# RMSNorm and matmul: x in a ring of 36 tiles, loaded twelve tiles at a time

## The chip, the core and the metric

The kernel runs on one core of a Trainium2 chip. The metric is the device time of one execution in microseconds (us), as the median of several runs; lower is better. A core has five engines with instruction streams of their own: TensorE (PE in the profile; PEld is its weight load), VectorE (DVE), ScalarE (ACT), GpSimd (POOL) and SyncE (SP, which only issues transfers here). 16 DMA engines move data between the chip's memory and the on-chip buffers (SBUF); the accumulators of TensorE are in PSUM.

## The reference

```python
batch, seq, dim, out_dim = 16, 1024, 512, 768        # x: float32, gamma: ones, eps: 1e-5
rms = np.sqrt(np.mean(x ** 2, axis=-1, keepdims=True) + eps)
x_norm = x / rms * gamma
return np.matmul(x_norm, weight).astype(np.float32)  # weight: [512, 768]
```

Each of the 16,384 rows of x is divided by its root mean square, scaled by gamma, and multiplied by the weight.

## The kernel before, in words

The rows are cut into 128 tiles of 128 rows (NT), taken in 64 pairs j (NP). A tile of x is 2 KB on each of the 128 partitions, a tile of the output 3 KB. The product is computed on the raw x in bf16, with gamma folded into the weight, and each output row is multiplied by its 1/rms when it leaves the accumulator.

Each tile goes through these steps:

- **Load** (`load`, L177). The first 32 tiles come on SP's queue in loads of 2, 2, 4, 8, 8 and 8 tiles, around the two halves of the weight (`load_weights`, L345). The later ones come on ScalarE's queue, 8 tiles (16 KB a partition) each. x has two buffers of 16 tiles, so a load overwrites tiles 32 places back and waits for their readers.
- **Cast** (`cast`, L188) on GpSimd, to bf16, in groups of up to 8 tiles, in `xb` (two buffers of 8 tiles). The last four tiles of each 16 (from tile 28 on) are a *quad*: `cast_quad` (L260) puts them in `xq`.
- **Turn.** TensorE transposes a tile as two blocks of 32-bit words against an identity (`transpose_word`, L230), into two PSUM banks; VectorE copies the result to `xT` (`evac`, L239). A quad is turned by 16 VectorE transposes (`move`, L271), three per pair from the pair after its cast on.
- **Norm.** ScalarE squares each tile and sums it (`square`, L196); a group's `root` is a square root on ScalarE (L201) and a reciprocal on VectorE (L203).
- **Product** (`matmuls`, L296 and L300): four weight loads and eight matmuls a tile, into one of three accumulators. A `feeder` puts the transposes of the pair after next between them.
- **Evict** (`finish_tile`): ScalarE (L279) takes the even tile of a pair and VectorE (L281) the odd one, into `ot`, three output buffers of 8 tiles. The last tile of a group is followed by its **store** (`store`, L293) on SP's queue. The first and last groups are stored in smaller pieces.

`Order` keeps the program's order on each engine and adds the semaphore waits that the named cells require. Every engine works in order, so an instruction that waits holds all that stand behind it. In the loop over pairs, pair j issues the casts of tiles some 8 to 16 places ahead, squares of pair j + 4, and the loads:

```python
if j == START or j > START and (j + LEAD) % 4 == 0:                          # START, LEAD = 4, 14
    load_until(2 * XG + OG if j == START else 2 * (j + LEAD) + OG)           # XG, OG = 16, 8
```

So from pair 6 on, every fourth pair issues the load of the eight tiles that begin at tile 2j + 28.

`rows` says which rows of x and the output a tile holds: within a block of t tiles, partition p holds t rows that lie next to each other in memory, one for each tile of the block. From tile 32 on the block is 32 tiles, so a partition's rows are 64 KB (x) or 96 KB (output) from the next partition's.

Of the kernel before, what the change touches and what calls it, by code (L numbers as in the profile page):

```python
# [11 lines left out]
F32 = mybir.dt.float32  # L12
BF16 = mybir.dt.bfloat16
AF = mybir.ActivationFunctionType


P = 128
# [83 lines left out]
def kernel(  # L101
# [9 lines left out]
    PE, DVE, ACT, POOL, SP = nc.tensor, nc.vector, nc.scalar, nc.gpsimd, nc.sync  # L111
    order = Order(tc)

    def run(engine, issue, reads=(), writes=()):
        order.add(1, engine, issue, reads, writes)

    x = x.flatten_outer_dims()
    out = out.flatten_outer_dims()
    N, D = x.shape
    _, O = out.shape  # L120
    K = D // P
    NT = N // P
    NP = NT // 2
    XG, OG = 16, 8
    FIRST, START, LEAD = 2 * XG, 4, 14

    def stretches(group, parts):
        first, size, i = {}, {}, 0
        for g in range(NT // group):
            for n in parts.get(g, [group]):  # L130
                for t in range(i, i + n):
                    first[t], size[t] = i, n
                i += n
        return first, size

    last = NT // OG - 1
    x_first, x_size = stretches(OG, {0: [2, 2, 4]})
    o_first, o_size = stretches(OG, {0: [1, 1, 2, 4], last - 1: [4, 4], last: [4, 2, 2]})

    def rows(ap, i, n):  # L140
        base, t = (i - i % OG, OG) if OG <= i < XG else (x_first[i], x_size[i]) if i < OG else (i - i % XG, XG) if i < 2 * XG else (i - i % (2 * XG), 2 * XG)
        return ap[base * P:(base + t) * P, :].rearrange("(p t) d -> p t d", t=t)[:, i - base:i - base + n, :]

    def sb(name, shape, dtype):
        return nc.alloc_sbuf_tensor(name, shape, dtype).ap()
# [5 lines left out]
    eps_sb = sb("eps_sb", [P, 1], F32)  # L151
    ident_f = sb("ident_f", [P, P], F32)
    g_sb = sb("g_sb", [P, 2, 2], F32)
    xt = [sb(f"xt{n}", [P, XG, D], F32) for n in range(2)]
    xb = [sb(f"xb{n}", [P, 8, D], BF16) for n in range(2)]
    jk = [sb(f"jk{n}", [P, D], BF16) for n in range(2)]
    xT = [sb(f"xT{n}", [P, 2, 2, P, 2], BF16) for n in range(4)]
# [1 line left out]
    xTq = [sb(f"xTq{n}", [P, 4, 2, P, 2], BF16) for n in range(2)]  # L159
    ot = [sb(f"ot{n}", [P, OG, O], F32) for n in range(3)]  # L160
    ssq = sb("ssq", [P, NT], F32)
    rms = sb("rms", [P, NT], F32)
    rstd = sb("rstd", [P, NT], F32)
    psum = nc.alloc_psum_tensor("ps", [P, 8 * WIDE], F32).ap()
    ops = [psum[:, 2 * WIDE * n:2 * WIDE * (n + 1)] for n in range(3)]
# [2 lines left out]
    def cells(name, slot, i, n=1):  # L168
        return [(name, slot, t) for t in range(i, i + n)]

    def x_of(i, n=1):
        return xt[i // XG % 2][:, i % XG:i % XG + n, :], cells("x", i // XG % 2, i % XG, n)

    def load(i):
        dst, to = x_of(i, x_size[i])
        queue = SP if i < FIRST else ACT
        order.transfer(queue, lambda: queue.dma_start(out=dst, in_=rows(x, i, x_size[i])), writes=to)  # L177
# [3 lines left out]
    def load_until(i):  # L181
        while starts and starts[0] < i:
            load(starts.pop(0))

    def cast(i, n=1):
        src, of = x_of(i, n)
        s = i // 8 % 2
        run(POOL, lambda: POOL.tensor_copy(out=xb[s][:, i % 8:i % 8 + n, :], in_=src), of, cells("xb", s, i % 8, n))  # L188
# [3 lines left out]
    def square(i):  # L192
        src, of = x_of(i)
        j = squares[0] % 2
        squares[0] += 1
        run(ACT, lambda: ACT.activation(out=jk[j], in_=src[:, 0, :], func=AF.Square, accum_out=ssq[:, i:i + 1]),  # L196
            of, [("jk", j), ("ssq", i)])

    def root(i, n):
        s = slice(i, i + n)  # L200
        run(ACT, lambda: ACT.activation(out=rms[:, s], in_=ssq[:, s], func=AF.Sqrt, scale=1.0 / D, bias=eps_sb),  # L201
            [("ssq", t) for t in range(i, i + n)] + ["eps"], [("rms", i)])
        run(DVE, lambda: DVE.reciprocal(out=rstd[:, s], in_=rms[:, s]), [("rms", i)],  # L203
            [("rstd", t) for t in range(i, i + n)])

    def norms(i, n):
        for t in range(n):
            square(i + t)
        root(i, n)
# [6 lines left out]
    def norms_of_group(j):  # L216
        square(2 * j)
        square(2 * j + 1)
        if j in norm_end:
            root(*norm_end[j])  # L220
# [33 lines left out]
    def quad_of(j):  # L254
        return j // 2 if (2 * j) % XG >= XG - 4 and 2 * j >= XG else None

    def cast_quad(q):
        src, of = x_of(4 * q, 4)
        s = 4 * q // XG % 2
        run(POOL, lambda: POOL.tensor_copy(out=xq[s], in_=src), of, [("xq", s)])  # L260
        for t in range(4):
            xT_of[4 * q + t] = (xTq[s][:, t], ("xTq", s))
        words = xq[s].rearrange("p t d -> p (t d)").bitcast(F32).rearrange("p (a w) -> p a w", w=P)
        turned = xTq[s].rearrange("p t h m c -> p (t h m c)").bitcast(F32).rearrange("p (a m) -> p a m", m=P)
        for tokens in range(0, P, B):
            for features in range(0, P, B):
                quad_moves.append((turned[features:features + B, :, tokens:tokens + B],
                                   words[tokens:tokens + B, :, features:features + B], s))
# [4 lines left out]
    def move_quad(n):  # L273
        for _ in range(min(n, len(quad_moves))):
            move(*quad_moves.pop(0))
# [9 lines left out]
    def accumulator():  # L285
        return next(turns) % 3

    def store(i):
        first, n = o_first[i], o_size[i]
        s = first // OG % 3  # L290
        if i == first + n - 1:
            src = ot[s][:, first % OG:first % OG + n, :]
            order.transfer(SP, lambda: SP.dma_start(out=rows(out, first, n), in_=src), reads=cells("ot", s, first % OG, n))  # L293
# [12 lines left out]
    def matmuls(i, a, ks, feed=None):  # L306
        block, cell = xT_of[i]
        for k in ks:
            lhsT = block[:, k // 2, :, k % 2]
            hold(lhsT, cell)  # L310
            for half, lo, hi in ((0, 0, WIDE), (1, WIDE, O)):
                product(ops[a][:, lo:hi], lhsT, w_bf[:, k, lo:hi], k == 0, k == K - 1,
                        [cell, ("w", k, half)], [("ops", a, half)])
            if feed:
                feed()

    def finish_tile(i, a, engine):
        s = i // OG % 3

        before = [("ot", s, i % OG - 1)] if i == o_first[i] + o_size[i] - 1 else []  # L320
        scale(engine, ot[s][:, i % OG, :], ops[a][:, :O], rstd[:, i:i + 1],
              [("ops", a, 0), ("ops", a, 1), ("rstd", i)] + before, [("ot", s, i % OG)])
        store(i)

    def feeder(pairs, gaps, alone=False):
        queue = [(j, t, h) for j in pairs for t in range(2) for h in range(2)]
        calls = iter(gaps)

        def feed():
            for _ in range(next(calls)):  # L330
                j, t, h = queue.pop(0)
                transpose_word(j, t, h)
                if alone and h == 1:
                    evac(j, t, 1)
                elif (t, h) == (1, 1):
                    evac(j)
        return feed
# [37 lines left out]
    for c in range(2):  # L375
        turn_gamma(c)
    run(DVE, lambda: DVE.tensor_copy(out=g_sb.rearrange("p c h -> p (c h)"), in_=tp[0][:, 0, 0, :4]), [("tp", 0)], ["g"])  # L377
    cast(0)
    cast(1)
    cast(2, 2)  # L380
    norms(0, 2)
    warm_up(2)
# [22 lines left out]
    for j in range(1, NP):  # L405
        if j in (1, 2):
            cast(4 * j + 4, 4)
        elif j % 8 == 4 and j + 4 < NP:
            cast(2 * j + 8, 8)
        elif j % 8 == 6 and j + 2 < NP:  # L410
            cast(2 * j + 12, 4)
        if (2 * j + 2) % XG == 0 and 2 * j + 2 < NT:
            cast_quad((2 * j + 2 + XG - 4) // 4)
        elif 2 * j >= XG:
            move_quad(3)
        if j < 4:
            norms(2 * j + 2, 2)
        for pair in norm_turns.get(j, []):
            norms_of_group(pair)
        if j == START or j > START and (j + LEAD) % 4 == 0:  # L420
            load_until(2 * XG + OG if j == START else 2 * (j + LEAD) + OG)
        if j < 3:
            feed = feeder([j + 1], mid if j == 1 else one, alone=j == 1)
        elif j == 3:
            feed = feeder([4, 5], both)
        elif j + 2 < NP and quad_of(j + 2) is None:
            feed = feeder([j + 2], two)
        else:
            feed = None
        for i, engine in ((2 * j, ACT), (2 * j + 1, DVE)):  # L430
            a = accumulator()
            matmuls(i, a, range(K), feed)
            finish_tile(i, a, engine)
# [48 lines left out]
```

## Time and profile before

| | |
|---|---|
| median of three runs | 208.84 us (208.83 to 209.33) |
| the profiled execution: its own time | 209.07 us |
| its span, first to last instruction | 207.1 us |
| granted TensorE clock | 0.993 |
| busy share: TensorE, VectorE, ScalarE, GpSimd | 94%, 72%, 70%, 29% |
| moved by DMA | 85.62 MB, 413 GB/s over the span |
| loads of x past tile 7: median from issue to landing | 18.2 us (3 on SP), 18.8 us (12 on ScalarE) |
| stores of 8 tiles, 3,072 KB: median from issue to landing | 22.7 us (13) |

The span is cut into 40 slices in the page's rows of digits; 9 is busy for 90% of a slice or more. In a list of groups or a timeline, a line names the engine, the line of the program, the operation, the tiles (out<-in) and how often; in brackets stands how long the engine was idle before, and what ended that. The name after an arrow in the list of waits is who was waited for, followed by the total in us, the number of waits and the longest. A DMA is split into packets; here one packet is one partition's row of a transfer, and each of the 16 DMA engines moves 8 of the 128.

### The profile page before, as it was taken

The page shows a single profiled execution, that of the slowest core. Times are in us where ns is not written, and L with a number is a line of the kernel's source. Part 1 is how long each engine was busy: PE and PEld are TensorE (multiplying, and loading weights), DVE is VectorE, ACT ScalarE, POOL GpSimd, SP SyncE. Part 2 cuts the span into 40 slices and gives each one's busy share as a digit, 9 for nine tenths or more (in the row PEclk, how much of TensorE's full clock was granted, in tenths as well). Part 3 has the DMA queues.
Part 4 walks back from the last instruction along what each step waited for, and adds up shares of the span by engine and source line. Part 5 has one row for each costly group of instructions (what it writes and reads, how often), then busy time and mean ns, then how long its engine had stood idle before and what let it go on. Part 6 is the DMA issues. An engine that isn't in the chain of part 4 may idle for free.

```text
span 207.1 us, 2794 instructions
## 1 busy us (share of the span) xinstructions
PE 194.7 (94%) x1236; PEld 72.7 (35%) x717; DVE 149.5 (72%) x255; ACT 144.3 (70%) x343; POOL 60.0 (29%) x34
## 2 busy tenths in 40 slices
PE   7789999999999999999999999999999989999940
PEld 1233434343334334433344333443343324333310
DVE  0446556999579975999579975999569964999530
ACT  4598898777777687777777687676949758683310
POOL 2156752157006340065105170060604224000000
PEclk9999999999999999999999999999999999999997
DMA  6999999999999999999999999999999999999992
GB/s 222 402 434 453 370 419 420 426 461 407 437 429 423 449 419 440 419 434 429 432 449 411 430 434 423 445 423 437 413 424 445 427 440 435 423 437 394 394 412 120
DMA packets 6064, 85.62 MB, mean 413 GB/s; under 512 B 674, under 2 KB 676, under 8 KB 1828
## 3 DMA queue, kind: packets, MB, share of 16 engines
q1 hardware_dynamic: 4320, 60.30, 68.9%
q10 hardware_dynamic: 1732, 25.17, 28.5%
q8 instruction: 7, 0.11, 0.2%
q14 instruction: 5, 0.04, 0.0%
HBM read 35.13 MB, written 50.33 MB: 413 GB/s over the span
## 4 chain that ended last, share of the span: by engine, by line
PE 71%; DMA 17%; DVE 5%; SPq 1%; issue 1%; POOL 1%; ACT 0%; ACTq 0%
PE ps L300 63%; DMA out_dram<-ot 12%; PE ps L230 8%; DMA xt<-in_x_dram 5%; DVE ot L281 2%; DVE xTq L271 2%; DVE xT L239 1%; POOL xb L188 1%; SPq L345 0%; ACT ot L279 0%; SPq L177 0%; DVE rstd L203 0%; SPq L477 0%; ACTq L93 0%; SPq L436 0%
## 5 line engine op out<-in xcount | busy, mean ns | idle before, releaser
L300 PE MATMUL ps<-w_bf,xT 128*128 128x512 bf16 (+1 forms) x800 | 147.9, 326 | 2.1 <-DVE w_bf L281 1.1
L279 ACT ACTIVATE ot<-ps,rstd 128x768 f32<-128x768 f32 x64 | 57.6, 899 | 48.5 <-PE ps L300 37.3
L196 ACT ACTIVATE jk<-xt 128x512 bf16<-128x512 f32 x128 | 78.7, 619 | 1.9 <-DMA xt<-in_x_dram 1.9
L188 POOL CAST xb<-xt 128x2048 bf16<-128x2048 f32 (+3 forms) x21 | 46.4, 2218 | 112.4 <-PE ps L230 69.0
L281 DVE TENSOR_SCALAR ot<-ps,rstd 128x768 f32<-128x768 f32 x64 | 64.8, 1013 | 9.5 <-PE ps L300 8.1
L296 PEld LDWEIGHTS <-xT 128*128 128x128 bf16 x400 | 39.3, 98 | 60.7 <-issue 52.8
L230 PE MATMUL ps<-ident_f,xb 128*128 128x128 f32 x200 | 54.4, 276 | 0.9 <-POOL xb L188 0.9
L239 DVE COPY xT<-ps 128x1024 bf16<-128x1024 bf16 (+1 forms) x53 | 34.5, 654 | 24.2 <-PE ps L230 22.5
L271 DVE STREAM_TRANSPOSE xTq<-xq 32x256 f32<-32x256 f32 x112 | 48.8, 435 | 3.4
L230 PEld LDWEIGHTS ps<-ident_f,xb 128*128 128x128 f32 x200 | 28.3, 143 | 46.6 <-issue 43.3
L300 PE MATMUL ps<-w_bf,xTq 128*128 128x512 bf16 x224 | 42.8, 326 | 0.0
L196 ACT ACTIVATION_READ_ACCUMULATOR jk<-xt 128x1 f32 x128 | 24.4, 190 | 0.0
L296 PEld LDWEIGHTS <-xTq 128*128 128x128 bf16 x112 | 11.0, 98 | 14.5 <-issue 14.5
L260 POOL CAST xq<-xt 128x2048 bf16<-128x2048 f32 x7 | 13.3, 1893 | 0.0
L203 DVE RECIPROCAL rstd<-rms 128x8 f32<-128x8 f32 (+3 forms) x20 | 3.9, 193 | 8.1 <-ACT rms L201 7.9
L201 ACT ACTIVATE rms<-ssq,eps_sb 128x8 f32<-128x8 f32 (+3 forms) x20 | 6.0, 300 | 0.6
L300 PE MATMUL ps<-warm 128*128 128x512 bf16 x10 | 4.5, 588 | 1.4 <-DVE eps_sb L354 1.4
L279 ACT ACTIVATE w_bf<-w_f,g_sb 128x768 bf16<-128x768 f32 x2 | 1.9, 935 | 1.8 <-DMA w_f<-in_weight_dram 1.8
L377 DVE COPY g_sb<-ps 128x4 f32<-128x4 f32 x1 | 0.2, 163 | 3.2 <-PE ps L371 3.2
L341 ACT ACT_TABLE_LOAD x1 | 1.3, 1283 | 1.5 <-SPq L436 1.5
L281 DVE TENSOR_SCALAR w_bf<-w_f,g_sb 128x512 bf16<-128x512 f32 (+2 forms) x3 | 1.4, 482 | 1.2 <-DMA w_f<-in_weight_dram 1.2
L371 PEld LDWEIGHTS ps<-ident_f,g_row 2*128 2x128 f32 x2 | 0.3, 200 | 2.6 <-issue 2.6
(10 smaller groups left out, 2.0 us busy)
## 6 DMA issues: line engine op xcount, KB each, us to landing
out_dram<-ot SPq DMA_DIRECT2D x13, 3072.0 KB, 22.7
xt<-in_x_dram ACTq DMA_DIRECT2D x12, 2048.0 KB, 18.8
xt<-in_x_dram SPq DMA_DIRECT2D x3, 2048.0 KB, 18.2
out_dram<-ot SPq DMA_DIRECT2D x4, 1536.0 KB, 10.9
out_dram<-ot SPq DMA_DIRECT2D x3, 768.0 KB, 6.8
w_f<-in_weight_dram SPq DMA_DIRECT2D x2, 768.0 KB, 5.9
xt<-in_x_dram SPq DMA_DIRECT2D x2, 512.0 KB, 5.4
xt<-in_x_dram SPq DMA_DIRECT2D x1, 1024.0 KB, 9.5
```

The lines of the kernel that those rows point to most:

```text
L188: run(POOL, lambda: POOL.tensor_copy(out=xb[s][:, i % 8:i % 8 + n, :], in_=src), of, cells("xb", s, i % 8, n))
L196: run(ACT, lambda: ACT.activation(out=jk[j], in_=src[:, 0, :], func=AF.Square, accum_out=ssq[:, i:i + 1]), of, [("jk", j), ("ssq", i)])
L201: run(ACT, lambda: ACT.activation(out=rms[:, s], in_=ssq[:, s], func=AF.Sqrt, scale=1.0 / D, bias=eps_sb), [("ssq", t) for t in range(i, i ...
L203: run(DVE, lambda: DVE.reciprocal(out=rstd[:, s], in_=rms[:, s]), [("rms", i)], [("rstd", t) for t in range(i, i + n)])
L230: run(PE, lambda: PE.transpose(out=tp[b][:, t, h, :], in_=words[:, lo:lo + P], identity=ident_f), cells("xb", s, j % 4 * 2 + t) + ["ident" ...
L239: run(DVE, lambda: DVE.tensor_copy(out=dst[:, t:t + n, :], in_=src[:, t:t + n, :]), [("tp", b)], cells("xT", j % 4, t, n))
L260: run(POOL, lambda: POOL.tensor_copy(out=xq[s], in_=src), of, [("xq", s)])
L271: run(DVE, lambda: DVE.transpose(out=dst, in_=src), [("xq", s)], [("xTq", s)])
L279: run(ACT, lambda: ACT.mul(out=dst, in_=src, mul=r), reads, writes)
L281: run(DVE, lambda: DVE.tensor_single_scalar(out=dst, in_=src, scalar=r, op=mybir.AluOpType.mult), reads, writes)
L296: run(PE, lambda: PE.ldweights(lhsT), [cell])
L300: run(PE, lambda: PE.add_instruction(mybir.InstMatmult(name=nc.get_next_instruction_name(), engine=mybir.EngineType.PE, ins=[PE.lower_ap(r ...
```

## The change

x is held in one buffer of 36 tiles, used as a ring, instead of two of 16. From tile 8 on it is loaded 12 tiles (24 KB a partition) at a time: the loads of 8 and 20 on SP's queue at the start, those from 32 on ScalarE's queue, each at the pair j at which its first tile is 2j + 28 (or in the first pair after it where that falls between pairs), and that of 32 at pair 4 as before. The blocks of rows change with it: from tile 8 on, all 120 tiles are one block, for x and the output alike, so a partition's rows are 240 KB (x) or 360 KB (output) from the next partition's. A cast whose tiles run past the end of the ring is cut in two. The buffer `rms` goes: the root is written in place of the sum of squares.

```diff
-    XG, OG = 16, 8
+    XG, OG, XL, RING = 16, 8, 12, 36
...
-    x_first, x_size = stretches(OG, {0: [2, 2, 4]})
+    x_first, x_size = {}, {}
+    for first, n in [(0, 2), (2, 2), (4, 4)] + [(i, XL) for i in range(OG, NT, XL)]:
+        for t in range(first, first + n):
+            x_first[t], x_size[t] = first, n
...
     def rows(ap, i, n):
-        base, t = (i - i % OG, OG) if OG <= i < XG else (x_first[i], x_size[i]) if i < OG else (i - i % XG, XG) if i < 2 * XG else (i - i % (2 * XG), 2 * XG)
+        base, t = (x_first[i], x_size[i]) if i < OG else (OG, NT - OG)
...
-    xt = [sb(f"xt{n}", [P, XG, D], F32) for n in range(2)]
+    xt = sb("xt", [P, RING, D], F32)
...
-    rms = sb("rms", [P, NT], F32)
...
     def x_of(i, n=1):
-        return xt[i // XG % 2][:, i % XG:i % XG + n, :], cells("x", i // XG % 2, i % XG, n)
+        at = (i + XL - OG) % RING
+        return xt[:, at:at + n, :], cells("x", 0, at, n)
...
     def cast(i, n=1):
+        ahead = RING - (i + XL - OG) % RING
+        if ahead < n:
+            cast(i, ahead)
+            return cast(i + ahead, n - ahead)
...
     def root(i, n):
         s = slice(i, i + n)
-        run(ACT, lambda: ACT.activation(out=rms[:, s], in_=ssq[:, s], func=AF.Sqrt, scale=1.0 / D, bias=eps_sb),
-            [("ssq", t) for t in range(i, i + n)] + ["eps"], [("rms", i)])
-        run(DVE, lambda: DVE.reciprocal(out=rstd[:, s], in_=rms[:, s]), [("rms", i)],
-            [("rstd", t) for t in range(i, i + n)])
+        sums = [("ssq", t) for t in range(i, i + n)]
+        run(ACT, lambda: ACT.activation(out=ssq[:, s], in_=ssq[:, s], func=AF.Sqrt, scale=1.0 / D, bias=eps_sb),
+            sums + ["eps"], sums)
+        run(DVE, lambda: DVE.reciprocal(out=rstd[:, s], in_=ssq[:, s]), sums, [("rstd", t) for t in range(i, i + n)])
...
-        if j == START or j > START and (j + LEAD) % 4 == 0:
-            load_until(2 * XG + OG if j == START else 2 * (j + LEAD) + OG)
+        if j >= START:
+            load_until(2 * XG + 1 if j == START else 2 * (j + LEAD) + 1)
```

## The prediction, made before the change was run

> **What bounds the kernel now.** I read the page first: which engine is full, and what the DMA engines do.
>
> ```profile
> PE   7789999999999999999999999999999989999940
> ...
> DMA  6999999999999999999999999999999999999992
> ...
> q1 hardware_dynamic: 4320, 60.30, 68.9%
> q10 hardware_dynamic: 1732, 25.17, 28.5%
> ```
>
> Two rows are full from the third slice on: TensorE and the 16 DMA engines (68.9 + 28.5 = 97.4% of the span). q1 is SP's queue (first loads, weights, all stores), q10 ScalarE's (the 12 later loads). Which of the two ends last? Busy time by stretch:
>
> ```profile
> core 0: us, PE busy (x) PEld busy (x) DVE busy (x) ACT busy (x) POOL busy (x), PEclk, DMA share, GB/s
> ...
> 42.00:142.00 100.00, 100.00 (x651) 37.85 (x375) 82.31 (x140) 74.54 (x178) 31.61 (x13) 1.00 1.01 431
> 142.00:168.00 26.00, 25.98 (x168) 9.64 (x96) 20.89 (x36) 17.25 (x42) 7.33 (x3) 1.00 1.00 428
> 168.00:190.00 22.00, 21.23 (x140) 8.12 (x81) 17.41 (x29) 16.04 (x39) 3.73 (x2) 1.00 1.00 430
> 190.00:200.00 10.00, 9.05 (x56) 2.64 (x27) 6.08 (x9) 3.59 (x4) 0.00 (x0) 1.00 0.94 393
> ```
>
> Both, to the end. TensorE loses 0.8 us after 142 us, when ScalarE finds no free output buffer; that is in the waits and in ScalarE's own timeline:
>
> ```profile
> ACT ot L279 <- DMA out_dram<-ot: 9.5, 4, 3.1
> ...
> PE ps L300 <- ACT ot L279: 0.8, 1, 0.8
> ```
>
> ```profile
> 168.01 0.90 ACT L279 ACTIVATE ot<-ps,rstd 128x768 f32<-128x768 f32 x1 [3.07 <-DMA out_dram<-ot]
> ```
>
> ScalarE waits 9.5 us for stores, but three accumulators cover all but 0.8 us of it. The end of the chain of waits:
>
> ```profile
> 188.32 10.74 PE ps L300 x66
> ...
> 199.09 1.02 DVE ot L281
> ```
>
> TensorE ends at 199.06 and the last store is issued at 200.40 (SP's timeline). How much of the tail is DMA backlog? The trace's packet records (queue, start, duration, size) tell. With an idle queue, the first packet follows the issue by 0.9 us (194.93 to 195.82). The last store is 8 packets per DMA engine of 6,144 bytes at 0.234 us, 1.9 us; the span ends 1.4 us after its last packet. Without backlog the span would end 1.34 + 0.9 + 1.9 + 1.4 = 5.5 us after TensorE, at 204.6. It ends at 207.06, because one DMA engine is 2.3 us behind the other fifteen (last packets at 205.7 and 203.4) and had no idle time. So **TensorE could end 2.5 us later and cost nothing**, while time taken out of the DMA work shows only as far as TensorE stays early.
>
> The start is the third view, GpSimd's timeline and the weight loads of TensorE:
>
> ```profile
> 12.52 2.02 POOL L188 CAST xb<-xt 128x1024 bf16<-128x1024 f32 x2 [1.44 <-DMA xt<-in_x_dram]
> 17.41 3.73 POOL L188 CAST xb<-xt 128x2048 bf16<-128x2048 f32 x2 [2.87 <-DMA xt<-in_x_dram]
> 22.38 3.60 POOL L188 CAST xb<-xt 128x4096 bf16<-128x4096 f32 x1 [1.23 <-DMA xt<-in_x_dram]
> 28.41 1.89 POOL L188 CAST xb<-xt 128x2048 bf16<-128x2048 f32 x1 [2.44 <-DMA xt<-in_x_dram]
> ```
>
> ```profile
> 19.36 0.14 PEld L230 LDWEIGHTS ps<-ident_f,xb 128*128 128x128 f32 x1 [0.37 <-POOL xb L188]
> ...
> 28.85 0.14 PEld L230 LDWEIGHTS ps<-ident_f,xb 128*128 128x128 f32 x1 [0.23 <-issue]
> ```
>
> The casts of tiles 8, 16 and 24 each wait for their load, and the first transpose of tile 8 (19.36) starts when its cast ends (17.41 + 1.89): no slack. The one at 28.85 is tile 16's, 2.9 us after its cast (22.38 + 3.60).
>
> **The change part by part.**
>
> *Packets.* Past tile 7, 15 loads of 8 packets per engine become 10. Load packets (16,384 bytes) have a median of 0.611 us, store packets of the new size (24,576 bytes) 0.912 us: 120 x 0.611 = 73.3 us becomes 80 x 0.912 = 73.0 us, and five completion packets of 9 ns go. DMA work: -0.4 us per engine, on a resource that is full throughout. That a load also pays something fixed is not seen: the first packet of a load (57.65) follows the end of the one before it (57.5) by 0.1 us. [...]
>
> *Row pitch in memory.* From tile 8 on, a partition's rows lie 240 KB apart in x and 360 KB in the output, instead of 16 to 64 KB and 96 KB. Loads at 16, 32 and 64 KB all have the same 0.611 us median, so I take zero. The nearest spread, 0.912 median against 0.915 mean for stores, gives 0.3%, 0.6 us either way.
>
> *The first loads.* SP's loads run in order, back to back. The load of 8 to 15 has its last completion packet at 16.94; the load of 8 to 19 replaces 8 x 0.611 = 4.88 us by 8 x 0.912 = 7.30 us, so tile 8 is there 2.4 us later and TensorE, without slack, waits 2.4 us. Next, the cast of tiles 16 to 23 is one instruction and now needs the load of 20 to 31, which ends when the load of 24 to 31 ended (27.5): it starts near 28.4, as the 28.41 row did, ends at 32.0 instead of 26.0, and is wanted at 28.9 + 2.4 = 31.3. Another 0.2 to 0.7 us; I take 0.6, since the landing is an observed one. Behind TensorE's wait are its own products, ScalarE's and VectorE's evictions and SP's stores. TensorE: **+3.0 us at 32 us**. The DMA engines are covered: stores of tiles 0 to 7 (7.5 us by their packets) and the load of 32 to 43 (7.3 us) last from 27.4 to 42.2, and the store of 8 to 15 is issued at 36.23 + 3.0 = 39.2.
>
> *Shares of the two queues.* While both have work, packets alternate: load and store cycles are 12.13 us, and 8 x (0.912 + 0.611) is 12.18. With 24 KB packets on both sides a load takes 8 x 1.82 = 14.6 us for 12 tiles, 1.22 us a tile instead of 1.52, so x gets ahead of the stores. [...] Were turns by byte, loads and stores would stand as before. Per 12 tiles the sum is unchanged: 20 packets, 18.2 us, against 1.5 x 12.13.
>
> *Where ScalarE's 9.5 us go.* TensorE, 3.0 us later, needs buffers 3.0 us later, about the longest of the single waits (1.6 to 3.1). But stores land later too: near 155 us the old queue had loaded x to tile 120, the new one to about 122, 2 x 0.61 = 1.2 us of DMA time ahead of the stores. By 169 us all loads are done in either kernel, so the store that frees tile 104's buffer (168.0) lands at most 1.1 us later, less the 0.4 saved. I take it that TensorE's 0.8 us stall goes and 0.2 us comes for store waits: TensorE ends 3.0 - 0.8 + 0.2 = 2.4 us late, 201.5.
>
> *Lateness of x.* Loads are issued 14 pairs ahead as before, mostly later than the old pieces but needed with them. The tightest are those starting with a quad (44, 92). Load 44: issue 35.5 + 3.0, first packet 3.9 us later (as 41.63 to 45.52), 14.6 us of packets, 2.0 us for the slowest engine and the signal, cast 1.89: 60.9. VectorE wants it at 59.54 + 3.0 = 62.5. Cover 1.6 us; beyond that VectorE, and TensorE behind its copies, wait one for one. On ScalarE the loads wait for casts that are over by eight pairs: zero.
>
> *At zero:* the root in place (20 instructions of 300 ns and 20 of 193 ns in both), and one cast of tiles 64 to 71 split in two (2 x 1.89 instead of 3.60 us, +0.2 us on GpSimd, which then waits for loads anyway).
>
> **Sum.** Against the profiled execution (span 207.06, 209.07 us in all; the median of the three runs is 208.84): the DMA side ends at 207.06 - 0.4 = 206.7; TensorE's side at 201.5 + 5.5 = 207.0. The later one decides: 207.0, no change worth the name. On the median: 208.8, and I put **208.9** for a few slow packets.
>
> **The rivals.**
>
> *Stores are crowded out (slower).* Loads go out on ScalarE's queue and take every other packet; a whole half load (6 tiles, 3.7 us) gets ahead of the stores when a buffer is due. Then the buffer for tile 96 (155.59) is free at 159.3; TensorE ends 3.5 us late, span 202.6 + 5.5 = 208.1, **209.9**. If it adds fully to the waits at the start: 3.0 + 3.5, span 211.1, 212.9. It decides from the point where TensorE ends more than 2.5 us late. For it: ScalarE already waits 9.5 us. Against: these waits and those at the start overlap. Chance 0.40, with the load-44 and load-92 lateness in it.
>
> *The slowest DMA engine falls back into step (faster).* If equal packets on both queues keep the 16 engines together, the 2.3 us lag goes; then TensorE decides: with the stall of 2.4 us alone less 0.8, 199.06 + 1.6 + 5.5 = 206.2, **208.0**. For it: the lag opens where 3 KB and 16 KB packets mix (27 to 33 us). Against: it grows again with stores alone (1.6 us at 142, 2.3 at 183). Chance 0.18.
>
> *Each load carries a fixed price.* If every load cost what lies around the last store's packets (0.9 + 1.4 us), five fewer would save 11.5 us, as far as TensorE allowed: 208.84 - 11.5 = 197.3. Against it is the 0.1 us between loads. Chance 0.04. [...]
>
> *Forecast, no change:* 0.38, its own range 208.3 to 209.5.
>
> **How the numbers follow.** 0.3% is 0.6 us, about what a measurement of this kernel can tell from no change. Faster 0.22, same 0.38, slower 0.40. The range runs from the faster rival, 208.0, to 211.2, short of the fully added case: DMA work bounds the low side, nothing bounds the high side as closely.
>
> **What would show it.** In the new profile: casts of tile 8 at 19.8 instead of 17.41, and of tile 16 at 28.4; two TensorE waits for GpSimd's casts, 3.0 us together; ScalarE's waits for stores well under 9.5 us; q10 and q1 together 0.4 us shorter; TensorE's end near 201.5. Wrong would be: packets of 24,576 bytes on q10 off 0.912 us; a DMA share under 1.0 between 30 and 190 us; waits of VectorE on casts near 62 or 132 us; TensorE ending after 202.2, or before 200.

## The result, and the profile after

The changed kernel is **slower by 1.1%**: median 211.65 us (13 runs, 210.19 to 213.66) against 209.06 us (13 runs, 208.57 to 210.65) for the kernel before on the same chip; ratio 1.0113, 95% interval 1.0092 to 1.0134. The profiled execution took 210.98 us (span 208.9) and so holds 1.9 us of the 2.6 to be explained; the changed kernel's runs also scatter more. All ratios leave out runs that are over 1.5% above the fastest of their kernel (among them 2 of these 13 and 3 of e12's 6 below), while medians and ranges hold every run.

The page of the changed kernel, full rows first, then the queues:

```profile
PE   7786999999999999999999999999996999999990
...
DMA  6999999999999999999999999999999999699787
...
q1 hardware_dynamic: 4176, 60.29, 68.6%
q10 hardware_dynamic: 1156, 25.17, 28.1%
```

The bytes are the same and so is the DMA work: summed over packets, 202.7 us per DMA engine against 202.4. New are three gaps: TensorE's slice 4, TensorE's slice 31, and the end of the DMA row, where 9s become 6s, 7s and 8s. The busy time by stretch of the changed kernel (columns as before):

```profile
core 0: us, PE busy (x) PEld busy (x) DVE busy (x) ACT busy (x) POOL busy (x), PEclk, DMA share, GB/s
...
20.00:26.00 6.00, 4.76 (x21) 2.13 (x15) 0.86 (x2) 4.53 (x13) 3.02 (x2) 0.72 1.05 365
...
142.00:168.00 26.00, 24.35 (x158) 9.18 (x91) 19.83 (x33) 17.25 (x43) 7.34 (x3) 1.00 1.01 427
168.00:190.00 22.00, 22.00 (x144) 8.35 (x83) 17.77 (x32) 17.46 (x42) 3.73 (x2) 1.00 0.92 392
190.00:200.00 10.00, 10.00 (x65) 3.29 (x34) 8.22 (x13) 3.27 (x4) 0.00 (x0) 1.00 0.76 317
```

Read the last two rows together: TensorE is busy without a gap while the DMA engines idle, 0.08 x 22 + 0.24 x 10 = 4.2 us of 32. Before, they idled 0.6 us there. TensorE is late, and the DMA engines run out of stores. Its two losses stand in the waits of the changed kernel:

```profile
ACT ot L286 <- DMA out_dram<-ot: 6.1, 2, 4.6
...
PE ps L237 <- POOL xb L195: 3.3, 3, 2.4
...
PE ps L307 <- ACT ot L286: 1.6, 1, 1.6
```

ScalarE waits less for stores than before (6.1 us against 9.5), but in two waits, one of 4.6 us. The accumulators cover only so much of a single wait, whatever the sum is. Before, ScalarE's wait for the buffer of tile 96 was covered whole, and the one of 3.07 us at 168.01 cost TensorE 0.8. In the changed kernel the wait for tile 96 is 1.63 us longer, and TensorE stands still for 1.65. The kernel before, then the changed kernel:

```profile
155.59 0.90 ACT L279 ACTIVATE ot<-ps,rstd 128x768 f32<-128x768 f32 x1 [2.98 <-DMA out_dram<-ot]
```

```profile
160.78 0.90 ACT L286 ACTIVATE ot<-ps,rstd 128x768 f32<-128x768 f32 x1 [4.61 <-DMA out_dram<-ot]
...
161.73 0.48 PE L307 MATMUL ps<-w_bf,xT 128*128 128x512 bf16 x2 [1.65 <-ACT ot L286]
```

The end of the chain of waits of the changed kernel goes back through that store:

```profile
133.46 27.23 DMA out_dram<-ot
160.78 0.91 ACT ot L286
...
192.57 10.74 PE ps L307 x66
203.34 1.02 DVE ot L288
```

The start is in GpSimd's and TensorE's timelines of the changed kernel. First the casts of tiles 8 to 15 and 16 to 23:

```profile
19.29 3.73 POOL L195 CAST xb<-xt 128x2048 bf16<-128x2048 f32 x2 [5.27 <-DMA xt<-in_x_dram]
27.97 5.44 POOL L195 CAST xb<-xt 128x4096 bf16<-128x4096 f32 x2 [4.95 <-DMA xt<-in_x_dram]
```

```profile
21.23 0.33 PE L237 MATMUL ps<-ident_f,xb 128*128 128x128 f32 x1 [2.36 <-POOL xb L195]
...
23.22 0.85 PE L307 MATMUL ps<-w_bf,xT 128*128 128x512 bf16 x2
...
26.11 0.49 PE L307 MATMUL ps<-w_bf,xT 128*128 128x512 bf16 x2
```

TensorE waits 2.36 us for tile 8. Then, from 22.16 to 25.57 us, the same pair of matmuls takes 0.85 us instead of 0.49; that is the granted clock of 0.72 in the row of 20 to 26 us.

**TensorE's account.** VectorE evicts every odd tile, so the same eviction in both traces gives TensorE's lateness at each. Here is the one of tile 81, in the kernel before and in the changed kernel:

```profile
131.91 1.01 DVE L281 TENSOR_SCALAR ot<-ps,rstd 128x768 f32<-128x768 f32 x1
```

```profile
135.46 1.01 DVE L288 TENSOR_SCALAR ot<-ps,rstd 128x768 f32<-128x768 f32 x1
```

The lateness is -0.53 us at tile 1 (TensorE is early), +3.55 from tile 7 to tile 91, +5.18 at tile 97, +4.25 from tile 109 to the end. The wait for tile 8 leaves TensorE 1.88 late (the wait, less the 0.53 by which it was early), the slower clock adds 1.67, the store wait 1.63, and stalls of 0.93 that the kernel before has are missing: 1.88 + 1.67 + 1.63 - 0.93 = 4.25. TensorE ends at 203.30 instead of 199.05, and the span 5.64 us later.

### The profile page after: what moved, and what is told of

It reads as the page before. It is cut to its first block, busy times and chain, and to the rows that moved or that the text cites. A ratio compares the mean times of both kernels' runs of the same rounds, so it can differ in the third digit from the quotient of the medians.

```text
span 208.9 us, 2778 instructions
## 1 busy us (share of the span) xinstructions
PE 195.9 (94%) x1236; PEld 73.1 (35%) x717; DVE 149.5 (72%) x255; ACT 144.6 (69%) x343; POOL 60.3 (29%) x35
## 4 chain that ended last, share of the span: by engine, by line
PE 73%; DMA 21%; SPq 1%; DVE 1%; POOL 1%; issue 1%; ACT 0%; ACTq 0%
PE ps L307 64%; DMA out_dram<-ot 13%; PE ps L237 8%; DMA xt<-in_x_dram 8%; DVE ot L288 1%; POOL xb L195 1%; SPq L180 1%; ACT ot L286 0%; SPq L352 0%; DVE xT L246 0%; SPq L484 0%; DVE xTq L278 0%; ACTq L93 0%; SPq L443 0%
## 5 line engine op out<-in xcount | busy, mean ns | idle before, releaser
L307 PE MATMUL ps<-w_bf,xT 128*128 128x512 bf16 (+1 forms) x800 | 149.4, 328 | 2.7 <-ACT ot L286 1.6
L288 DVE TENSOR_SCALAR ot<-ps,rstd 128x768 f32<-128x768 f32 x64 | 64.8, 1013 | 10.2 <-PE ps L307 7.7
L211 DVE RECIPROCAL rstd<-ssq 128x8 f32<-128x8 f32 (+3 forms) x20 | 3.8, 192 | 8.3 <-ACT ssq L209 8.1
L209 ACT ACTIVATE ssq<-ssq,eps_sb 128x8 f32<-128x8 f32 (+3 forms) x20 | 6.0, 301 | 0.6
## 6 DMA issues: line engine op xcount, KB each, us to landing
out_dram<-ot SPq DMA_DIRECT2D x13, 3072.0 KB, 21.1
```

The costliest lines, as they stand in the source:

```text
L209: run(ACT, lambda: ACT.activation(out=ssq[:, s], in_=ssq[:, s], func=AF.Sqrt, scale=1.0 / D, bias=eps_sb), sums + ["eps"], sums)
L211: run(DVE, lambda: DVE.reciprocal(out=rstd[:, s], in_=ssq[:, s]), sums, [("rstd", t) for t in range(i, i + n)])
L288: run(DVE, lambda: DVE.tensor_single_scalar(out=dst, in_=src, scalar=r, op=mybir.AluOpType.mult), reads, writes)
L307: run(PE, lambda: PE.add_instruction(mybir.InstMatmult(name=nc.get_next_instruction_name(), engine=mybir.EngineType.PE, ins=[PE.lower_ap(r ...
```

## The experiments

Two things had to be told apart: the **late start** (tile 8 comes with a larger load, and the clock falls) and what the **larger loads** do to the stores and to x later on. The quoted expectations give the theories short names; for the later part they went from stores crowded out, over x that is late because whole loads must land, to the **balance** of the two queues. Ratios are against the kernel before on the same chip. Lateness is TensorE's at the end, read off VectorE's evictions in the profiled execution.

### Is it the ring, the rows or the root?

The changed kernel with loads of 8 in a ring of 32 (`e4_ring_of_eights`):

```diff
-    XG, OG, XL, RING = 16, 8, 12, 36
+    XG, OG, XL, RING = 16, 8, 8, 32
```

> The changed kernel with XL = 8 and RING = 32: loads of 8 into 32 tiles as before, but all 120 tiles one block of rows (240 KB and 360 KB from partition to partition), the root in place and the casts cut at the ring's end. Theories 'start' and 'shares': as the kernel before, 208.8 to 209.3, 24,576-byte packets at 0.912 us and 16,384-byte ones at 0.611 us. If the pitch of the rows costs: longer packets and 210 to 211.6.

Measured: 208.96 us against 209.04, ratio 0.9990 (0.9970 to 1.0010), TensorE 0.03 us early. The ring, the rows 240 KB and 360 KB apart and the root in place cost nothing that can be seen. A ring of 32 has no split cast; that one costs nothing either, since TensorE's lateness in the changed kernel stays at 3.55 us past tiles 64 to 71. What is left is the size of the loads.

### The late start

First four tiles after tile 8 by themselves (`e1_first_four`), so that tile 8 is early again:

```diff
-    for first, n in [(0, 2), (2, 2), (4, 4)] + [(i, XL) for i in range(OG, NT, XL)]:
+    for first, n in [(0, 2), (2, 2), (4, 4), (8, 4), (12, 8)] + [(i, XL) for i in range(OG + XL, NT, XL)]:
```

> The changed kernel, with its load of tiles 8 to 19 cut in one of 4 tiles (8 to 11) and one of 8 (12 to 19); all from tile 20 on is as changed. Theory 'start': the loss comes from TensorE's wait of 2.4 us for tile 8 and the lower clock behind it (1.7 us). Tile 8 is then there before it is wanted: no wait at 19 us, granted clock 1.00 in 20 to 26 us, TensorE at 42 us no later than in the kernel before, and the time back at 208.5 to 209.2. Theory 'shares': 24 KB load packets push the stores back, whatever the start: no wait at 19 us either, but ScalarE's waits for stores grow past 9.5 us and TensorE loses 2 us or more to them; time 210.5 to 212.

Measured: 211.38 us, ratio 1.0105 (1.0072 to 1.0137). The wait did not go but moved: TensorE waits 4.3 us, up to 32.6, for the cast of tiles 16 to 23, which needs the load of 20 to 31, with a granted clock of 0.89 from 26 to 42 us, and ends 4.28 us late. This tells nothing of what an early start is worth.

The wait filled with matmuls that change no output (`e2_filled_gap`), ahead of pair 3's own products:

```diff
+        if j == 3:
+            hold(warm[:, :P], "warm")
+            for _ in range(11):
+                product(ops[1][:, :WIDE], warm[:, :P], warm, True, True, ["warm"], [("ops", 1, 0)])
```

> The changed kernel, with 11 matmuls on the constant warm-up tile (0.21 us each, 2.4 us) put in front of the products of tile 6, into an accumulator that is free; they fill TensorE's wait for tile 8 and change no output. If the lower clock from 22 to 25.5 us follows from the idle time: granted clock 1.00 there, TensorE 1.7 us earlier at 42 us than in the changed kernel, and 1.0 to 1.7 us off the time (210.0 to 210.6), less if store waits take it back. If the clock falls for another reason: no change, 211.6.

Measured: 211.28 us, ratio 1.0091 (1.0057 to 1.0125), against 1.0113 for the changed kernel, with intervals that overlap. Filling the wait is worth little if anything.

The late start alone, in the kernel before (`e3_before_late_tile8`): tiles 16 to 19 are loaded ahead of 8 to 15, so that tile 8 is as late as after the change.

```diff
-    x_first, x_size = stretches(OG, {0: [2, 2, 4]})
+    x_first, x_size = stretches(OG, {0: [2, 2, 4], 2: [4, 4]})
...
+    starts.remove(16)
+    starts.insert(3, 16)
```

> The kernel before (two buffers of 16, loads of 8, rows as they were), with the load of 16 to 23 cut in two of 4 and the first of these put ahead of the load of 8 to 15: tile 8 comes 2.4 us later, as in the changed kernel, and nothing else changes. Theory 'start': TensorE waits 2.4 us, runs at a lower clock for some 3 us, is 3.5 to 4 us late at 42 us, and the time is 210.5 to 212. Theory 'shares': 208.8 to 209.5, since the late TensorE is taken up by the waits for stores and by the tail.

And the same with the eleven matmuls in the wait (`e6_late_tile8_filled`, the lines of e2 added to e3):

> The kernel before with tile 8 late by 2.4 us (as in the run of that name), and 11 matmuls on the constant warm-up tile in TensorE's wait; no output changes. It parts the wait from the lower clock behind it. If the clock falls because TensorE idles: granted clock 1.00 in 20 to 26 us, TensorE 1.9 us late at 42 us instead of 3.6 to 3.8, which the 2.5 us of slack at the end cover: 208.8 to 209.2 instead of 210.0. If the clock falls anyway: 210.0.

Measured: 210.00 us, ratio 1.0037 (1.0006 to 1.0069), and 210.28 us, ratio 1.0046 (1.0027 to 1.0066). The stretch from 20 to 26 us, of e3 and then of e6:

```profile
20.00:26.00 6.00, 4.53 (x20) 2.03 (x14) 0.86 (x2) 4.57 (x15) 6.00 (x3) 0.72 1.05 416
```

```profile
20.00:26.00 6.00, 5.87 (x38) 2.24 (x23) 2.09 (x4) 4.66 (x15) 6.00 (x3) 1.00 1.06 404
```

With the wait filled the clock stays at 1.00 and TensorE is 2.0 us late after it instead of 3.79: the fall of the clock follows the idle time and is worth 1.8 us of TensorE. But the whole time isn't better for it. In e6's profile TensorE ends 1.08 us late and the span is 1.16 longer: the DMA engines end later too. The span still ends 8.1 us after TensorE, and the last store lands on its slowest engine 2.6 us after the fastest, as in the kernel before. A late start alone costs about 1.0 us, not 2.6.

### The larger loads without the late start

The changed kernel with the old first loads, twelves from tile 32 only (`e5_old_start`):

```diff
-    for first, n in [(0, 2), (2, 2), (4, 4)] + [(i, XL) for i in range(OG, NT, XL)]:
+    for first, n in [(0, 2), (2, 2), (4, 4), (8, 8), (16, 8), (24, 8)] + [(i, XL) for i in range(FIRST, NT, XL)]:
```

> The changed kernel with the first loads as they were (2, 2, 4, then 8, 8 and 8 tiles up to tile 31); the ring and the loads of 12 from tile 32 on are as changed. This parts the two theories, which the load of 4 and 8 tiles did not, since the wait only moved to tile 16. Theory 'start': TensorE has no wait before 32 us and a granted clock of 1.00 there; at 42 us it is where the kernel before has it; time 208.5 to 209.2. Theory 'shares': TensorE, early now, loses 1.5 us or more to waits for stores between 60 and 170 us; time 210 to 211. If both hold, the store waits here are larger than in the changed kernel and the time lies between: about 209.8.

Measured: **213.48 us**, ratio 1.0185 (1.0151 to 1.0219), slower than the changed kernel itself. TensorE is 0.34 us early up to tile 43, then 2.18 late at tile 49, 4.6 at 79, 7.57 at 97. Its waits:

```profile
ACT ot L286 <- DMA out_dram<-ot: 18.6, 6, 5.2
...
DVE ot L288 <- DMA out_dram<-ot: 5.8, 4, 2.4
PE ps L307 <- ACT ot L286: 5.8, 4, 2.3
```

Part of this is the clock again: behind the wait of 2.27 us that ends at 88.19, the granted clock is 0.50 from 89.38 to 92.79. So the store waits, with what follows them, are the larger cost, and the late start hides part of them. The costs do not add: 1.0 alone (e3), 4.6 alone (e5), 2.6 together. Three traces line up on this. After the start TensorE is 0.34 us early in e5, 3.55 late in the changed kernel and 5.39 late in e1; its later waits behind ScalarE are 5.8, 1.6 and none; and a store of 3,072 KB takes a median of 24.5, 21.1 and 18.8 us to land.

### All loads on one queue

If turns between two queues make the stores late, one queue ends them. `queue = SP` for all loads, in e5 (`e7_old_start_one_queue`), in the changed kernel (`e8_changed_one_queue`) and in the kernel before (`e9_before_one_queue`):

```diff
-        queue = SP if i < FIRST else ACT
+        queue = SP
```

> The run with the old start and loads of 12 from tile 32 on, with all loads on SP's queue: loads and stores stand in one queue in the order of the program and no packets alternate. Theory 'alternation': what costs is that a 24 KB load takes every other packet (14.6 us for a store instead of 12.2), in a different phase on each DMA engine, so that a store's last engine is up to 10 us behind its first. Then here the spread from first to last engine stays under 3 us, the waits for stores fall from 24.4 us to under 10 and the time from 213.5 to 208.5 to 209.8. Rival 'lumps': a load of 12 in front of a store costs the same 7.3 us in one queue; the waits for stores stay over 15 us and the time over 211.

> The changed kernel with all loads on SP's queue. 'Alternation': what is left is the price of the late start, 1.0 us as in the kernel before with a late tile 8, so 209.5 to 210.2 instead of 211.65. 'Lumps': no better than 211.

> The kernel before with all loads on SP's queue: loads of 16 KB and stores of 24 KB one after the other. In two queues they alternate in a steady pattern, 12.1 us for one of each. If the pattern is what keeps the engines in step there, one queue does no worse and the slowest engine's lag of 2.3 us at the end may shrink: 208.0 to 209.3. If the two queues are needed to keep stores from waiting behind loads: 210 or more.

Measured: e7 211.06 us, ratio 1.0100 (1.0085 to 1.0116); e8 211.48, ratio 1.0116 (1.0102 to 1.0130); e9 209.55, ratio 1.0021 (1.0010 to 1.0033). In e7 the waits for stores are gone, 2.4 us of e5's 4.6 come back, and x is late in their place: GpSimd waits 69.7 us for x ahead of its casts and 23.6 ahead of the quads', and TensorE ends 4.55 us late. e8 is no better than the changed kernel. So without turns the stores are no longer late, but a large load that stands in line with the stores makes x late instead. The load of tile 44 goes out at 35.97 us in e7; in e9, the load of tile 40 went out at 25.9. That this is all of it was not tried.

### Later or smaller loads

If x only comes too early, loads can go out later (`e10_old_start_later_loads`: e5 with `LEAD` 12 for 14), or in DMAs half the size, so that a store gets a larger share (`e11_old_start_two_halves` from e5, `e12_changed_two_halves` from the changed kernel):

```diff
-        dst, to = x_of(i, x_size[i])
         queue = SP if i < FIRST else ACT
-        order.transfer(queue, lambda: queue.dma_start(out=dst, in_=rows(x, i, x_size[i])), writes=to)
+        n = x_size[i] if i < FIRST else XL // 2
+        for t in range(i, i + x_size[i], n):
+            dst, to = x_of(t, n)
+            order.transfer(queue, lambda dst=dst, t=t: queue.dma_start(out=dst, in_=rows(x, t, n)), writes=to)
```

> The run with the old start and loads of 12 from tile 32 on (213.5), with LEAD 12 instead of 14: each load from tile 44 on is issued two pairs, 6 us, later. Theory 'x too early': at full DMA, loads of x that nobody needs yet take the time of stores that somebody waits for. In that run the load of 44 to 55 landed near 49 us and was first wanted at 59, so 6 us later is still in time; waits for stores fall from 24.4 us to under 15, TensorE gains 2 to 4 us, time 210 to 212. Rival 'shares alone': what counts is every other packet while a load runs, whenever that is; waits over 20 us and 213 to 214. If x comes too late instead: waits of VectorE and TensorE for GpSimd's casts, 214 or more.

> The run with the old start and loads of 12 (213.5), with each load from tile 32 on issued as two DMAs of 6 tiles, one right behind the other: the same bytes at the same pairs, but packets of 12,288 bytes (0.46 us) instead of 24,576. A store in a load's way then takes 8 x (0.91 + 0.46) = 11.0 us instead of 14.6. Theory 'shares': waits for stores fall from 24.4 us to under 10, and the time to 209 to 210.5. Rival 'lumps' (what counts is that 12 tiles are asked for at once): 212.5 or more, waits as before.

> The changed kernel with each load from tile 32 on issued as two DMAs of 6 tiles. 'Shares': its store waits (7.9 us in the profiled run) go, and what is left is the price of a late start, some 1 us: 209.8 to 210.5 instead of 211.65. 'Lumps': 211.5.

Measured: e10 212.39 us, ratio 1.0158 (1.0132 to 1.0183); e11 214.35, ratio 1.0242 (1.0212 to 1.0273); e12 216.15, ratio 1.0254 (1.0210 to 1.0297). None of the three has waits for stores that matter, and all are slow: GpSimd waits for x (74.5 us in e10, 67.3 in e11), and TensorE behind it. The relief that was looked for from halves went the other way. A next guess was that x is late because a whole load of 12 must land; loads of 4 in the ring of 36 (`e13_ring_of_fours`) would mend that:

```diff
-    XG, OG, XL, RING = 16, 8, 12, 36
+    XG, OG, XL, RING = 16, 8, 4, 36
```

> The changed kernel with XL = 4: the ring of 36 tiles stays, each load from tile 8 on is 4 tiles (packets of 8,192 bytes, 0.31 us) and is issued when its own first tile is 28 ahead. Theory 'whole loads': with 12 tiles a load, x must be brought up to 11 tiles further than its first tile, and TensorE waits for all 12; the 6 + 6 kernels kept that and were slow. Here it goes, so TensorE ends within 1 us of the kernel before and the time is 208.6 to 209.8. Theory 'packet sizes' (anything but 16 KB against 24 KB upsets the two queues): loads get a still smaller share of a shared DMA engine than with 12,288-byte packets, x comes late as there, and the time is 212 or more.

Measured: 213.64 us, ratio 1.0230 (1.0202 to 1.0258). That guess fell too. The waits of e13:

```profile
POOL xb L195 <- DMA xt<-in_x_dram: 88.1, 13, 18.3
...
PE ps L307 <- DVE ot L288: 4.4, 4, 1.8
```

### Balance

What the loads of 12, 6 and 4 have in common is that they aren't as many tiles as a store. While both queues have work, every DMA engine takes a packet from each in turn, eight from a load and eight from a store (in the kernel before, 12.13 us for a load and a store). So in the same time one load and one store are done, whatever their sizes. With the median packets of the traces (4, 6, 8, 12 tiles of x: 0.309, 0.460, 0.611, 0.912 us; 4 and 8 of the output: 0.460 and 0.912), the pace while both have work is:

| load / store, tiles | kernel | us per tile of x | us per tile stored | last load ends at | median us |
|---|---|---|---|---|---|
| 8 / 8 | before, e4 | 1.52 | 1.52 | 168.1, 169.5 | 209.0, 209.0 |
| 12 / 8 | changed, e5 | 1.22 | 1.82 | 162.0, 163.0 | 211.7, 213.5 |
| 6 / 8 | e11 | 1.83 | 1.37 | 178.2 | 214.4 |
| 4 / 8 | e13 | 2.44 | 1.22 | 180.2 | 213.6 |
| 4 / 4 | e14 | 1.54 | 1.54 | 170.1 | 210.4 |
| 8 / 4 | e15 | 1.07 | 2.14 | 165.1 | 211.3 |

(First row: 8 x (0.611 + 0.912) / 8 tiles = 1.52.) TensorE takes 1.46 us per tile (23.42 us for 16 tiles, by VectorE's evictions at 75.68 and 99.10 in the kernel before). Only 8 / 8 and 4 / 4 give x and output nearly that pace at once. The packet records of one DMA engine from 70 us on show the turns (S a store's packet, l a load's, a dot the end of a DMA). The records don't name the engine; a row is put together by laying packets end to start, so the pattern counts and not each letter:

```
before  lSlSlSlSlSlSl.lS.SlSlSlSlSlSlSl.lS.SlSlSlSlSlSlSl.lS.SlSlSl
changed SlSlS.SSlSlSl.lSlSlSlSlS.SSS.SSSlSlSlSlSlSl.lSlS.S
e13     lSlSl.ll.lllllllSlS.SlSlSlSlSlSl.ll.llSlSlSlSlSlSlS.Sl.lllllll.llllllll
e15     l.lSlSlSlSlSlSlS.S.SlSlSlSlSlSlSlSl..SSSSSSSSl.lSlSlSlSlSlSlS.S.SSSSSSSS
```

Before, one alternates with the other throughout. Everywhere else the queue with more tiles per DMA gets ahead while they alternate, runs out of what it may do, and the other follows alone: stores in the changed kernel and in e15, loads in e13.

The last two rows of the table are the test, kernels chosen after the others had been run. Balance restored at another size (`e14_fours_both_ways`, e13 with stores of 4 as well):

```diff
-    o_first, o_size = stretches(OG, {0: [1, 1, 2, 4], last - 1: [4, 4], last: [4, 2, 2]})
+    o_first, o_size = stretches(OG, {**{g: [4, 4] for g in range(1, last)}, 0: [1, 1, 2, 4], last: [4, 2, 2]})
```

> The ring with loads of 4 tiles (213.6), with the stores of the middle groups cut to 4 tiles too: packets of 8,192 bytes for x and 12,288 for the output, so that a turn of the two queues moves as many tiles of x as of the output, as in the kernel before (8 and 8). Theory 'balance': what upsets the kernel is any other number of tiles in a load than in a store (12 to 8: stores late; 6 to 8 and 4 to 8: x late). Then TensorE's waits for x go and the time is 208.5 to 210. If small loads are late for another reason (their packets, their number): x is as late as with stores of 8, 213 or more.

and balance broken in the kernel before, with nothing of the change in it (`e15_before_stores_of_four`, the same line):

> The kernel before with the stores of the middle groups cut to 4 tiles and nothing else changed: loads of 8, stores of 4. 'Balance': loads now outrun stores by 8 tiles to 4, more than the 12 to 8 of the changed kernel; waits for stores appear early and grow past 9.5 us, and the time is 210.5 to 213, with no part of the change in it. If it is not the balance: 208.5 to 209.3, or a little less, since buffers come free in halves.

Measured: e14 **210.38 us**, ratio 1.0057 (1.0035 to 1.0080), just above the 210 expected, 3.3 us faster than e13 through smaller stores; e15 **211.26 us**, ratio 1.0098 (1.0073 to 1.0124), 2.3 us slower through the same smaller stores. Two stretches of e14, the last stretch of e15, then the waits of e15:

```profile
42.00:142.00 100.00, 100.00 (x650) 37.77 (x375) 82.30 (x140) 74.95 (x179) 32.98 (x14) 1.00 1.01 427
...
190.00:200.00 10.00, 7.24 (x45) 2.05 (x21) 4.51 (x5) 2.70 (x3) 0.00 (x0) 1.00 1.01 428
```

```profile
190.00:200.00 10.00, 10.00 (x65) 3.37 (x34) 8.34 (x14) 3.16 (x4) 0.00 (x0) 1.00 0.72 301
```

```profile
ACT ot L279 <- DMA out_dram<-ot: 12.5, 5, 3.9
...
PE ps L300 <- ACT ot L279: 4.1, 2, 2.5
```

In e14 TensorE never waits from 42 to 190 us, ends 1.8 us early, and the DMA share is 1.01 to the end: what makes it slower than the kernel before is then DMA work (203.9 us per engine against 202.4, in more and smaller packets). e15 has the changed kernel's picture, with a DMA share of 0.72 from 190 to 200 us and TensorE 4.36 us late. The Trainium skill, "DMA: Bandwidth & Descriptors", section "Queues, rings and completion order", has each engine go round its queues packet by packet. The rows of turns agree: one packet of each in turn, of 0.309 and 0.912 us in e13, of 0.611 and 0.460 us in e15.

No version here beats the kernel before; e4 equals it.

## Why the prediction was wrong, step by step

**The cause.** The DMA engines are full, so x that comes early is paid for by stores that come late. The last load ends 6.1 us earlier than before, and nobody needs it then. The stores that were passed over hold an output buffer, ScalarE can't evict, TensorE stops, and a lost microsecond of TensorE isn't made up, since it runs without a gap to the end. The DMA engines, ahead on loads, then wait for outputs that TensorE can't make faster. The same work is done, with idle time near the end.

- *Packets*: 24,576 bytes on the load queue have a median of 0.912 us, as taken. The DMA work did not fall by 0.4 us (202.7 against 202.4), which decides nothing here.
- *Row pitch* and *At zero*: right, by e4 and, for the split cast, by the constant lateness past tile 64.
- *The first loads*: the casts came at 19.29 and 27.97 us (19.8 and 28.4 forecast), the wait at 2.36 us (2.4 forecast). The term was still 0.55 us short, 3.55 for 3.0. It lacked the clock's fall after the wait (1.67 us). Against that, it counted 0.6 us for the cast of tiles 16 to 23, which cost nothing because TensorE was that late already, and TensorE came to the wait 0.53 us earlier than in the trace before.
- *Shares of the two queues*: the paces were right (1.22 us a tile for x), and the step said that x gets ahead of the stores. It then closed with an unchanged sum of DMA work. That sum was true and answered the wrong question: who waits is set by the order, not by the sum.
- *Where ScalarE's 9.5 us go*: **this step failed**. It took 0.2 us for store waits, and the profiled execution shows 1.63; with the start's 0.55 and the old stalls at 0.93 instead of 0.8 that makes 4.25 us of lateness instead of 2.4 (2.4 + 0.55 + 1.43 - 0.13). The step set TensorE's 3.0 us of lateness against the waits, and then priced the store that frees tile 104's buffer. That one did cost nothing: it landed at 169.18 instead of 167.93, and no wait came of it. The store before it, which frees tile 96's buffer, was not priced. Lateness gave nothing back there, because this store goes out late by the same 3.55 us (133.46 instead of 129.91). And it took 27.23 us to land instead of 25.60: by the packet records, loads held a DMA engine for 12.9 us of that time, on average, and for 10.2 before. The wait of 2.98 us, just covered before, became 4.61, and the 1.63 us more went through to TensorE. So the sum of waits fell as forecast (6.1 us), and the cost rose.
- *Lateness of x*: right for this kernel, no wait of VectorE on the casts of the quads. In the kernels with one queue or smaller loads it became the cost.
- *The end*: right for this execution. TensorE's end + 5.5 us gives 208.8 for a span of 208.9, and with 2.5 us of lateness free, 4.25 us cost 1.8. As a rule the 2.5 us do not hold: in e6, 1.08 us of lateness cost 1.16.
- *What would show it*: two of the signs of being wrong came, TensorE's end after 202.2 (203.30) and a DMA share under 1.0 before 190 us (0.92 from 168 to 190).

Of the rivals, *Stores are crowded out* is what happened. Its argument against itself, that these waits overlap with those at the start, holds for the time (e3, e5). Its 209.9 us was too low: it had tile 96's buffer free at 159.3, and it was free at 160.69, by 3.55 us of late start and 1.63 of a slower store. The faster rival didn't come: the store of 133.46 lands on its first and last engine 5.1 us apart, and the same store before 2.9. Nor did the fixed price of a load: five fewer loads leave the DMA work where it was.

**What stays open.** The profiled execution accounts for 1.9 us; why other runs of the changed kernel take up to 213.7 us is not shown by one trace. Each run may catch a different store on the wrong side of a load, as in e5, but that is argued, not shown. One trace of a near kernel points that way: e2's profiled run, its longest at 213.56 us, has a store wait of 6.1 us on ScalarE that becomes 3.17 us on TensorE, with a granted clock of 0.50 for 3.41 us right behind it.

## What to carry to other kernels

When the DMA engines are full and two queues share them, look at how many units of work one DMA of each queue carries, not only at bytes or counts. Where the queues took turns here, the kernels with equal numbers (8 / 8, 4 / 4) were the fastest, and a larger DMA on one side worked as a priority over the other. Ask of any earlier transfer what becomes later in its place and whether someone waits for that. And judge waits by the longest one against the cover, not by their sum.

## What the runs showed of the hardware that had not been expected

- **The clock falls after a short wait.** 2.36 us without a matmul, and for 3.4 us (22.16 to 25.57) a pair of matmuls took 0.85 us instead of 0.49. The same half clock, for 3.4 us, follows waits of 2.27 us in e5 and 2.48 us in e15; the wait of 1.65 us at 161.73 in the changed kernel has none behind it. The Trainium skill, "TensorE: Matmul & The Clock Gate", section "Part 1: The HAM clock gate", puts half the clock behind an idle window of some 3.4 us, which runs free of the kernel. The length of the slow stretch agrees with that window; the idle time that set it off here is shorter.
- **Turns are by packet, whatever its size.** While a DMA of 4 tiles and one of 8 on the other queue share the engines (e13, e15), each gets one packet in turn; the side with the smaller packets doesn't get more turns.
- **The DMA engines drift apart.** A store of e5 was done on its last engine 10.6 us after its first (138.5 to 149.1 us), against 2.6 us for the same store in the kernel before, where from 42 us on no store has more than 4.0. ScalarE's wait ends only when the last engine is done. In the store that cost the changed kernel 1.63 us, the engines took 0.6 us longer on average and the last one 1.6, so the drift is part of the loss; how large a part was not isolated.
